# Residual tiles of both token halves kept on chip between output projection and channel mixer

## The chip, the cores and the metric

The kernel runs on one core of one Trainium2 chip. The metric is the device time of one execution in microseconds (us). Before the change three timed runs took 2567.0, 2571.26 and 2571.03 us, a median of 2571.03 us.

The engines are PE (TensorE, matrix products), DVE (VectorE), ACT (ScalarE), POOL (GpSimd) and SP (SyncE, which here only issues DMA transfers). Each engine works through its own list of instructions in order, and waits for the others by semaphores.

## The reference

A decoder trunk of two layers on one sequence of 1024 tokens with 1024 features, all in fp32. Each layer adds a token mixer and then a channel mixer to the residual stream `x`:

```
for layer in (0, 1):
    n = rms_norm(x, g1)
    x = x + mixer(n) @ w_out          # layer 0: dilated + forgetting attention, layer 1: differential attention
    n = rms_norm(x, g2)
    gate, up = split(n @ w_up, 2)     # 2816 columns each
    x = x + (silu(causal_conv3(gate)) * up) @ w_down
return rms_norm(x, g)
```

The change touches the two places where `x + mixer(n) @ w_out` ends and `rms_norm(x, g2)` begins.

## The kernel before

Activations lie transposed: a tile holds 128 features by 512 tokens. So the residual stream is eight feature tiles times two halves of the tokens (half 0 and half 1), 256 KB each. Every fp32 product is made of three matmuls, with operands split into a high and a low part (`mm3`, L150). Weights come in through `wget` (L119): a raw piece is loaded by SP into one of two `wr` slots, ACT makes the high part (`wh`, L129), DVE the low part (`wl`, L131). `split` (L162) does the same for activations, on ACT (L165) and DVE (L166). `put` (L193) is a load issued by SP, `store` (L196) a store issued by POOL; both queues work in order.

The order of the instructions comes from a scheduler: attention units and jobs of a list `J0` are woven together, and the tile pools decide by their slots when a tile can be filled.

`out_jobs` makes the jobs of the output projection. Its first job sums the first four head tiles into both token halves, the second job adds four more for half 0, and the job `rest` adds three more for half 1. After each product L1162 adds it to a residual tile `rt`, which had been loaded from DRAM (`parts`, `hp` in the traces), and POOL stores the tile there again. When half 0 is done, `stats` makes the norm's factors, and `blocks` loads the eight tiles of half 0 again (`t0`, `t<-hp`), multiplies each by the norm's factors (`token_blocks`, L1118 to L1121, an instruction at L1120), stores it to `half0` (`nt`) and splits it into `nh` and `nl`, the operands of the channel mixer.

`channel` is the channel mixer. It first adds the last head tile for half 1: eight products in a PSUM tile `dn`, added by L1364 to eight tiles `x` that are loaded from `parts` (`wq<-hp`). Each sum goes through `norm_chunk` (squares at L238, added up at L250) and is stored again (`hp<-wq`). `norm_cols` sums over the features with `ones` on PE (`small<-ones,sc`), `norm_rows` spreads the factor over the tokens (`dg`, `small<-dg`, `rb`). Then L1120 norms half 1, and L1384, L1385, L1393 and L1395 form the sums and differences with `b0`, the stored blocks of half 0, from which `cut` makes the split operands `bt` of the other block products (the up projection is done by seven block products in place of eight). Between these steps `lead` puts pieces of the gate product, whose sums ACT moves to `sc` (L931), POOL stores to `e` and SP loads again as `sc<-e` and `g<-e`. POOL also makes sums of raw up-projection weights in place (L824).

The channel mixer's pool has sixteen `wq` slots: before, `x` takes eight, `b0` four, and raw weights the rest; four more tiles of `b0` lie in `bt` slots. The pool `big` has 32 slots for `rt`, `t0`, `nh`, `nl`, the head tiles and others.

## Time and profile before

| | |
|---|---|
| median of three runs | 2571.03 us (2567.0 to 2571.26) |
| the profiled execution | 2565.89 us, of which its span takes 2564.1 us |
| mean granted TensorE clock | 0.983 of full speed |
| busy in the span | PE 96%, DVE 77%, ACT 48%, POOL 28% |
| DMA | 536.96 MB, 209 GB/s on average |

The profile is of one execution, 5.14 us shorter than the median. Its times count from the start of the span. A busy share is an average over the whole span; the passages between the stages are only seen in windows and timelines. In a timeline a row has its start, its length, the engine, line, operation, tiles and count, and in brackets how long the engine stood idle before it and what ended that.

### The profile page before, as it was taken

Reading aid. Unit: us, or ns where it says so; the run is one execution under the profiler, and the core shown is the slowest. Engines: PE = TensorE matmul, PEld = TensorE weight load, DVE = VectorE, ACT = ScalarE, POOL = GpSimd, SP = SyncE. Lnnn points to the kernel's source line nnn. Section 1 sums busy time; section 2 is a strip of 40 time slices with the busy share of each in tenths; the row PEclk is TensorE's granted clock in tenths of the full one; section 3 lists DMA queues with packets and bytes.
Section 4 is the critical chain, followed back from the end, with each engine's and each line's share of the span. In section 5 each row is a group of like instructions: output and inputs, shape, how many; then the busy total and the mean of one; then the engine's idle time right before and its main releaser. Section 6 shows DMA issues by size and latency. Waiting matters only on the chain.

```text
span 2564.1 us, 38450 instructions
## 1 busy us (share of the span) xinstructions
PE 2467.2 (96%) x12511; PEld 2047.6 (80%) x12511; DVE 1979.0 (77%) x3885; ACT 1221.5 (48%) x2443; POOL 721.4 (28%) x978
## 2 busy tenths in 40 slices
PE   8999999998899999999999999989888999999998
PEld 7899898776688888778888888877666888887886
DVE  7778878776988988775666888878769878977656
ACT  5456655454544344454434555545454443435433
POOL 1211112222444665100021211232225456740000
PEclk9999999998999999999999999999989999999998
DMA  5655556867766887664555555696576677766644
GB/s 192 229 172 172 178 173 216 255 204 275 216 207 219 244 241 240 205 220 167 193 202 169 197 182 193 203 288 216 179 253 198 204 238 242 248 201 231 226 130 160
DMA packets 249240, 536.96 MB, mean 209 GB/s; under 512 B 37976, under 2 KB 50896, under 8 KB 249040
## 3 DMA queue, kind: packets, MB, share of 16 engines
q1 hardware_dynamic: 179792, 320.02, 39.3%
q0 software_dynamic: 68672, 213.96, 25.1%
q8 instruction: 99, 1.62, 0.3%
q14 instruction: 101, 0.83, 0.1%
q10 hardware_dynamic: 576, 0.52, 0.1%
HBM read 362.33 MB, written 172.03 MB: 208 GB/s over the span
## 4 chain that ended last, share of the span: by engine, by line
PE 79%; DVE 8%; DMA 7%; ACT 3%; issue 2%; SPq 0%; POOL 0%; DVEq 0%; ACTq 0%; POOLq 0%
PE pj L145 67%; PE D L145 5%; PE O L145 4%; PE T L148 3%; DVE wl L131 2%; DMA wr<-in_wgate 1%; DVE bt L166 1%; PE small L145 1%; DMA wr<-in_wdown 1%; ACT wh L129 1%; DVE e L590 1%; DMA ncb<-cd 1%; ACT e L739 1%; DMA wr<-in_wqkC 1%; DMA ar<-td 1%
## 5 line engine op out<-in xcount | busy, mean ns | idle before, releaser
L145 PE MATMUL pj<-bt,wh 128*128 128x512 f32 x1760 | 554.2, 395 | 13.0 <-DVE bt L166 8.6
L145 PEld LDWEIGHTS pj<-bt,wh 128*128 128x128 f32 x1760 | 331.2, 188 | 93.5 <-DVE bt L166 11.6
L131 DVE TENSOR_TENSOR wl<-wr,wh 128x512 fp32r<-128x512 f32 (+2 forms) x340 | 235.7, 696 | 180.8 <-ACT wh L129 171.1
L145 PE MATMUL pj<-nh,wh 128*128 128x512 f32 x864 | 356.9, 413 | 16.8 <-ACT nh L232 8.6
L129 ACT ACTIVATE wh<-wr 128x512 fp32r<-128x512 f32 (+2 forms) x340 | 211.4, 624 | 290.5 <-PE pj L145 122.5
L145 PE MATMUL pj<-bt,wl 128*128 128x512 f32 x880 | 347.7, 395 | 0.0
L145 PE MATMUL pj<-nl,wh 128*128 128x512 f32 x864 | 346.2, 401 | 0.0
L145 PE MATMUL pj<-nh,wl 128*128 128x512 f32 x864 | 346.0, 401 | 0.0
L131 DVE TENSOR_TENSOR wl<-wq,wh 128x512 fp32r<-128x512 f32 x268 | 278.0, 1038 | 30.4 <-ACT wh L129 30.2
L129 ACT ACTIVATE wh<-wq 128x512 fp32r<-128x512 f32 x268 | 166.7, 628 | 239.2 <-PE pj L145 186.9
L824 POOL TENSOR_TENSOR wq<-wq 128x512 f32<-128x512 f32 x132 | 195.3, 1491 | 211.4 <-DVE wl L131 102.3
L145 PE MATMUL pj<-ah,wh 128*128 128x512 f32 (+1 forms) x628 | 248.0, 396 | 2.5 <-ACT s L1086 1.2
L145 PE MATMUL pj<-ah,wl 128*128 128x512 f32 (+1 forms) x628 | 246.2, 393 | 0.0
L145 PE MATMUL pj<-al,wh 128*128 128x512 f32 (+1 forms) x628 | 246.1, 392 | 0.0
L145 PEld LDWEIGHTS pj<-nh,wh 128*128 128x128 f32 x864 | 166.1, 192 | 49.9 <-ACT nh L232 8.6
L165 ACT ACTIVATE ph<-T 128x512 fp32r<-128x512 f32 (+3 forms) x288 | 138.9, 486 | 131.5 <-PE T L148 128.7
L145 PEld LDWEIGHTS pj<-bt,wl 128*128 128x128 f32 x880 | 165.8, 188 | 39.0
L145 PEld LDWEIGHTS pj<-nh,wl 128*128 128x128 f32 x864 | 165.5, 192 | 37.9 <-DVE wl L131 0.4
L145 PEld LDWEIGHTS pj<-nl,wh 128*128 128x128 f32 x864 | 166.2, 192 | 31.1 <-DVE nl L247 0.5
L166 DVE TENSOR_TENSOR pl<-T,ph 128x512 fp32r<-128x512 f32 (+3 forms) x288 | 157.5, 552 | 34.2 <-ACT ph L165 32.9
L148 PE MATMUL T<-ident,e 128*128 128x128 f32 x864 | 144.1, 277 | 19.2 <-DVE e L746 13.5
L145 PE MATMUL pj<-wh,nh 128*128 128x256 f32 (+1 forms) x512 | 149.0, 293 | 0.0
(476 smaller groups left out, 5339.7 us busy)
## 6 DMA issues: line engine op xcount, KB each, us to landing
wq<-in_wgate SPq DMA_DIRECT2D x88, 256.0 KB, 3.7
wq<-in_wup SPq DMA_DIRECT2D x88, 256.0 KB, 3.9
act<-v POOLq DMA_DIRECT2D x44, 512.0 KB, 3.6
td<-sc POOLq DMA_DIRECT2D x80, 256.0 KB, 4.5
wq<-in_wdown SPq DMA_DIRECT2D x80, 256.0 KB, 4.4
sd<-wq POOLq DMA_DIRECT2D x80, 256.0 KB, 4.1
ar<-td SPq DMA_DIRECT2D x80, 256.0 KB, 3.8
wr<-sd SPq DMA_DIRECT2D x80, 256.0 KB, 3.8
```

Of the source, the lines that this page charges most:

```text
L129: nc.scalar.activation(hi[:, :n], raw[:, :n], AF.Copy)
L131: nc.vector.tensor_tensor(lo[:, :n], raw[:, :n], f(hi[:, :n]), ALU.subtract)
L145: self.last = self.nc.tensor.matmul(*args, **kw)
L148: self.last = self.nc.tensor.transpose(*args)
L165: nc.scalar.activation(hi, src, AF.Copy)
L166: nc.vector.tensor_tensor(lo, src, f(hi), ALU.subtract)
L590: self.nc.vector.tensor_tensor_reduce(out=e[:, k0:k0 + w], in0=d[:, :w], in1=in1(k0, w), scale=1.0, scalar=init, op0=ALU.add, op1=ALU.min, ...
L739: nc.scalar.activation(e[m][:, :W], e[m][:, :W], AF.Exp, scale=-1.0, bias=nm[:, m:m + 1], accum_out=ls[:, m, i4:i4 + 1])
L824: nc.gpsimd.tensor_tensor(dst, x, y, op)
```

## The change

The tiles of both halves stay in SBUF. For half 0 the results of the second job are kept as `t0` and used by `blocks` directly; their store to `parts` stays. For half 1 the results of `rest` are kept as `self.t1[l]`, are no longer stored there, and are the `x` of `channel`. The eight tiles `b0` now all lie in `wq` slots. In each layer sixteen loads and eight stores of 256 KB go away; no arithmetic is added or removed. Lines behind the edit move by two, so L1162 becomes L1164, and L1364 becomes L1362.

```diff
-            def add(src, norm):
+            def add(src, keep=None):
...
-                    self.store(parts[l][m][:, cs[half]], t)
-                    if norm:
-                        self.norm_chunk(st, m, half, t, None)
+                    if half == 0 or keep is None:
+                        self.store(parts[l][m][:, cs[half]], t)
+                    if keep is not None:
+                        keep[m] = t
+                        if half == 0:
+                            self.norm_chunk(st, m, half, t, None)
                 return b, e
...
             def blocks():
-                ts = []
-                for m in range(10):
+                rest.fetch()
+                for m in range(9):
                     if m < 8:
-                        t = f(self.big.tile([P, HT], F32R, name="t0", tag="big"))
-                        self.put(t, parts[l][m][:, cs[0]])
-                        ts.append(t)
-                    if m == 0:
-                        rest.fetch()
-                    if 0 < m < 9:
-                        self.token_blocks(st, gi, 0, m - 1, ts[m - 1])
-                        self.store(half0[m - 1], ts[m - 1])
-                    if m > 1:
+                        self.token_blocks(st, gi, 0, m, t0[m])
+                        self.store(half0[m], t0[m])
+                    if m > 0:
                         hl = (self.big.tile([P, HT], F32R, name=x, tag="big") for x in ("nh", "nl"))
...
-            jobs += [self.job_out(w, [4, 5, 6, 7], [0], O, *add(part, True), 29 if l == 0 else 13)]
-            rest = self.job_out(w, [4, 5, 6], [1], O, *add(part, False), 27 if l == 0 else 14, 3)
+            jobs += [self.job_out(w, [4, 5, 6, 7], [0], O, *add(part, t0), 29 if l == 0 else 13)]
+            rest = self.job_out(w, [4, 5, 6], [1], O, *add(part, self.t1[l]), 27 if l == 0 else 14, 3)
...
-            x = [wq() for _ in range(8)]
-            for m in range(8):
-                self.put(x[m], parts[l][m][:, cs[1]])
+            x = [self.t1[l][m] for m in range(8)]
...
-            b0 = [wq() for _ in range(4)] + [f(small()) for _ in range(4)]
+            b0 = [wq() for _ in range(8)]
```

On SP's queue, at the start of layer 0's channel mixer, the lines with a minus are those of before (`hp` is the residual in DRAM, `nt` the stored blocks of half 0, `in_wgate` the gate weights):

```order
 L194 DMA cw<-in_cw 128x88
-L194 DMA wq<-hp_0_127 128x512
+L194 DMA wq<-nt_171 128x512
 L127 DMA wr<-in_wgate 128x512 x2
-L194 DMA wq<-hp_1_128 128x512
-L194 DMA wq<-hp_2_129 128x512
-L194 DMA wq<-hp_3_130 128x512
-L194 DMA wq<-hp_4_131 128x512
-L194 DMA wq<-hp_5_132 128x512
-L194 DMA wq<-hp_6_133 128x512
-L194 DMA wq<-hp_7_134 128x512
```

The reloads are gone and the first of the eight loads of half 0's blocks stands ahead of the first two weight pieces. Behind the blocks, before:

```order
L127 DMA wr<-in_wgate 128x512 x2
L194 DMA sc<-e_0_151 128x512
L194 DMA g<-e_1_152 128x512
L194 DMA wq<-in_wgate 128x512
L194 DMA wq<-in_wup 128x512
L127 DMA wr<-in_wgate 128x512 x2
```

And at the same place now:

```order
L127 DMA wr<-in_wgate 128x512 x2
L194 DMA wq<-in_wgate 128x512
L194 DMA wq<-in_wup 128x512 x2
L127 DMA wr<-in_wgate 128x512
L194 DMA sc<-e_0_151 128x512
L127 DMA wr<-in_wgate 128x512 x4
L194 DMA g<-e_1_152 128x512
```

Five weight pieces moved ahead of the load `g<-e_1_152`, and three raw weights ahead of the fifth piece.

On DVE, from the last residual adds of layer 0's channel mixer to its first L1120, before:

```order
L250 TENSOR_TENSOR sc_8020<-sc_8020,sc_8082 128x512
L178 TENSOR_SCALAR rq_x_8154<-small_8149 128x4
L183 TENSOR_TENSOR rq_z_8156<-rq_y_8155 128x4
L184 TENSOR_TENSOR rq_z_8156<-rq_z_8156,rq_x_8154 128x4
L185 TENSOR_SCALAR rq_z_8156<-rq_z_8156 128x4
L187 TENSOR_TENSOR rc_7487<-rq_y_8155,rq_z_8156 128x4
L131 TENSOR_TENSOR wl_8106<-wr_8102,wh_8104 128x512
L131 TENSOR_TENSOR wl_8127<-wr_8123,wh_8125 128x512
L273 TENSOR_SCALAR dg_8209<-ident_558,rc_7487 128x128 x4
L966 SCALAR_TENSOR_TENSOR pj_8663<-g_8146,cw_7953,pj_8663 128x512 x2
L1120 SCALAR_TENSOR_TENSOR wq_7999<-wq_7999,gn_69,rb_7503 128x512
```

The same stretch now:

```order
L250 TENSOR_TENSOR sc_7980<-sc_7980,sc_8042 128x512
L178 TENSOR_SCALAR rq_x_8114<-small_8109 128x4
L131 TENSOR_TENSOR wl_8129<-wr_8125,wh_8127 128x512
L183 TENSOR_TENSOR rq_z_8116<-rq_y_8115 128x4
L184 TENSOR_TENSOR rq_z_8116<-rq_z_8116,rq_x_8114 128x4
L185 TENSOR_SCALAR rq_z_8116<-rq_z_8116 128x4
L187 TENSOR_TENSOR rc_7487<-rq_y_8115,rq_z_8116 128x4
L131 TENSOR_TENSOR wl_8151<-wr_8147,wh_8149 128x512
L273 TENSOR_SCALAR dg_8169<-ident_558,rc_7487 128x128 x4
L131 TENSOR_TENSOR wl_8183<-wr_8179,wh_8181 128x512
L1120 SCALAR_TENSOR_TENSOR rt_7532<-rt_7532,gn_69,rb_7503 128x512
```

The convolution (L966) left the stretch for a place behind L1120, and the fifth, sixth and seventh weight splits since the start of the adds stand in it, where the third and fourth stood.

On DVE, where layer 1's first half is normed between the attention's last units (`e<-D` are logits, `pl` split probabilities), before:

```order
L1120 SCALAR_TENSOR_TENSOR t0_20492<-t0_20492,gn_69,rb_20468 128x512
L166 TENSOR_TENSOR nl_20497<-t0_20480,nh_20496 128x512
L166 TENSOR_TENSOR pl_20465<-T_20609,ph_20464 128x4x128
L166 TENSOR_TENSOR nl_20505<-t0_20488,nh_20504 128x512
L590 ISA e_20618,nm_20616<-D_20634,strip_14245,mn_20632 128x384
L590 ISA nm_20616 128x1
L166 TENSOR_TENSOR nl_20513<-t0_20492,nh_20512 128x512
L1120 SCALAR_TENSOR_TENSOR t0_20500<-t0_20500,gn_69,rb_20468 128x512
```

The end of the same run now:

```order
L1120 SCALAR_TENSOR_TENSOR rt_20080<-rt_20080,gn_69,rb_20428 128x512
L166 TENSOR_TENSOR nl_20469<-rt_20053,nh_20468 128x512
L1120 SCALAR_TENSOR_TENSOR rt_20119<-rt_20119,gn_69,rb_20428 128x512
L166 TENSOR_TENSOR nl_20475<-rt_20055,nh_20474 128x512
L1120 SCALAR_TENSOR_TENSOR rt_20172<-rt_20172,gn_69,rb_20428 128x512
L166 TENSOR_TENSOR nl_20481<-rt_20080,nh_20480 128x512
L166 TENSOR_TENSOR pl_20425<-T_20553,ph_20424 128x4x128
L166 TENSOR_TENSOR nl_20487<-rt_20119,nh_20486 128x512
L590 ISA e_20562,nm_20560<-D_20578,strip_14205,mn_20576 128x384
```

All eight L1120 and seven of the eight splits now stand ahead of the logits that before came after three L1120 and two splits; the run begins, as before, right behind another L590.

## Rows read from the trace of the kernel before

**Rows 1.** The page's busy times, with each engine's share of the span.

```profile
PE 2467.2 (96%) x12511; PEld 2047.6 (80%) x12511; DVE 1979.0 (77%) x3885; ACT 1221.5 (48%) x2443; POOL 721.4 (28%) x978
```

**Rows 2.** Windows: stretch, length, busy time per engine, clock, DMA share, GB/s.

```profile
579.00:593.00 14.00, 10.84 (x58) 8.50 (x58) 13.67 (x25) 8.78 (x18) 5.93 (x11) 0.94 0.82 289
614.00:650.00 36.00, 29.37 (x118) 22.46 (x116) 21.44 (x41) 16.78 (x30) 8.86 (x15) 0.91 0.88 314
650.00:695.00 45.00, 39.21 (x155) 30.08 (x156) 44.42 (x54) 24.79 (x45) 21.57 (x23) 0.92 0.71 211
700.00:1000.00 300.00, 300.00 (x1295) 243.09 (x1294) 262.04 (x352) 121.74 (x199) 173.56 (x190) 1.00 0.74 229
1819.00:1836.00 17.00, 9.65 (x47) 6.85 (x46) 16.72 (x39) 10.04 (x25) 5.93 (x11) 0.83 0.53 192
1868.00:1906.00 38.00, 29.51 (x110) 22.23 (x110) 21.11 (x39) 17.85 (x31) 10.94 (x17) 0.87 0.86 307
1906.00:1950.00 44.00, 39.28 (x159) 30.77 (x158) 43.79 (x58) 24.52 (x45) 18.25 (x20) 0.92 0.65 203
```

**Rows 3.** Timeline of SyncE's queue, both passages: start, length, line, transfers issued.

```profile
615.61 0.98 SPq L127 DMA_DIRECT2D wr<-in_wgate  x2
616.64 4.83 SPq L194 DMA_DIRECT2D wq<-hp  x7
...
628.54 1.78 SPq L127 DMA_DIRECT2D wr<-in_wgate  x2
...
640.58 0.33 SPq L194 DMA_DIRECT2D g<-e  x1
...
641.97 0.84 SPq L127 DMA_DIRECT2D wr<-in_wgate  x2
...
1871.22 0.86 SPq L127 DMA_DIRECT2D wr<-in_wgate  x2
...
1883.99 1.02 SPq L127 DMA_DIRECT2D wr<-in_wgate  x2
```

**Rows 4.** DMA, 612 to 640: GB/s in 40 slices, then issues with us to landing.

```profile
GB/s 0 0 0 0 0 84 185 287 222 307 266 255 249 307 389 395 389 418 395 407 398 407 404 418 410 410 416 407 404 418 398 415 407 407 398 445 386 395 366 220
...
wq<-hp SPq DMA_DIRECT2D x8, 256.0 KB, 6.6
...
wr<-in_wgate SPq DMA_DIRECT2D x4, 256.0 KB, 10.5
```

**Rows 5.** Timeline of DVE, both passages; idle time before in brackets.

```profile
619.30 0.69 DVE L1364 TENSOR_TENSOR wq<-wq,pj 128x512 f32<-128x512 f32 x1 [3.52 <-DMA wq<-hp]
...
630.02 2.27 DVE L250 TENSOR_TENSOR sc<-sc 128x512 f32<-128x512 f32 x3
...
645.62 1.83 DVE L1120 SCALAR_TENSOR_TENSOR wq<-wq,gn,rb 128x512 f32<-128x512 f32 x1
...
1873.96 0.69 DVE L1364 TENSOR_TENSOR wq<-wq,pj 128x512 f32<-128x512 f32 x1 [2.48 <-DMA wq<-hp]
...
1886.11 2.27 DVE L250 TENSOR_TENSOR sc<-sc 128x512 f32<-128x512 f32 x3
...
1905.13 2.24 DVE L1120 SCALAR_TENSOR_TENSOR wq<-wq,gn,rb 128x512 f32<-128x512 f32 x2 [1.24 <-ACT rb L282]
```

**Rows 6.** Timeline of PE: column sums of layer 0, norm stretch of layer 1.

```profile
632.48 1.80 PE L145 MATMUL small<-ones,sc 128*128 128x1 f32 x8
...
1831.30 0.87 PE L148 MATMUL T<-ident,e 128*128 128x128 f32 x3 [4.46 <-DVE e L746]
```

**Rows 7.** Timeline of DVE where layer 1's first half is normed.

```profile
1819.74 2.07 DVE L1120 SCALAR_TENSOR_TENSOR t<-t,gn,rb 128x512 f32<-128x512 f32 x3
...
1823.53 0.61 DVE L590 CUSTOM_DVE_ANT_0 e<-D,strip,mn 128x384 f32<-128x384 f32 x1
```

**Rows 8.** Timelines of DVE and of POOL (GpSimd), layer 1's channel mixer.

```profile
1933.19 5.33 DVE L166 TENSOR_TENSOR bt<-wq,bt 128x512 fp32r<-128x512 f32 x1
...
1933.81 4.15 POOL L824 TENSOR_TENSOR wq<-wq 128x512 f32<-128x512 f32 x3
```

More of the change, by code (lines that the diff above doesn't have):

```diff
@@ L1149, in run @@
         cs = [slice(hf * HT, (hf + 1) * HT) for hf in range(2)]
+        self.t1 = {}
         def out_jobs(l, w, base):
             st, gi, O = stF[l], 2 * l + 1, Os[l]
-            def add(src, norm):
+            def add(src, keep=None):
                 def b(m, half):
@@ L1174, in blocks @@
             def blocks():
-                ts = []
-                for m in range(10):
+                rest.fetch()
+                for m in range(9):
                     if m < 8:
-                        t = f(self.big.tile([P, HT], F32R, name="t0", tag="big"))
-                        self.put(t, parts[l][m][:, cs[0]])
-                        ts.append(t)
-                    if m == 0:
-                        rest.fetch()
-                    if 0 < m < 9:
-                        self.token_blocks(st, gi, 0, m - 1, ts[m - 1])
-                        self.store(half0[m - 1], ts[m - 1])
-                    if m > 1:
+                        self.token_blocks(st, gi, 0, m, t0[m])
+                        self.store(half0[m], t0[m])
+                    if m > 0:
                         hl = (self.big.tile([P, HT], F32R, name=x, tag="big") for x in ("nh", "nl"))
-                        st["h"][m - 2, 0], st["l"][m - 2, 0] = hl
-                        self.split(st["h"][m - 2, 0], st["l"][m - 2, 0], ts[m - 2])
+                        st["h"][m - 1, 0], st["l"][m - 1, 0] = hl
+                        self.split(st["h"][m - 1, 0], st["l"][m - 1, 0], t0[m - 1])
                 yield 0.0
+            t0, self.t1[l] = {}, {}
             last = lambda k: 4 * k + 3 if l == 0 else 2 * k + 1
@@ L1193, in out_jobs @@
             jobs = [self.job_load(O, k, last(k)) for k in range(4)]
-            jobs += [self.job_out(w, [0, 1, 2, 3], [0, 1], O, *add(base, False), last(3))]
+            jobs += [self.job_out(w, [0, 1, 2, 3], [0, 1], O, *add(base), last(3))]
             jobs += [self.job_load(O, k, last(k)) for k in range(4, 6)]
-            jobs += [self.job_out(w, [4, 5, 6, 7], [0], O, *add(part, True), 29 if l == 0 else 13)]
-            rest = self.job_out(w, [4, 5, 6], [1], O, *add(part, False), 27 if l == 0 else 14, 3)
+            jobs += [self.job_out(w, [4, 5, 6, 7], [0], O, *add(part, t0), 29 if l == 0 else 13)]
+            rest = self.job_out(w, [4, 5, 6], [1], O, *add(part, self.t1[l]), 27 if l == 0 else 14, 3)
             jobs += [Job(stats, 1.3), Job(blocks, 0.0)]
```

## The prediction

> **What bounds the kernel now.** I read the page's busy times first. PE is busy for 96% of the span [rows 1], so only places where PE waits or runs at a low clock can give anything; the reader should look for those places, not at totals. The windows show where they are not: from 700 to 1000, inside a channel mixer, PE is busy all 300 us at a granted clock of 1.00, with 1295 matmuls, that is 0.232 us each [rows 2]. They are at the two passages from a mixer to its channel mixer. Layer 0: 6.6 of 36 us idle from 614 to 650 (36.00 − 29.37) and 5.8 of 45 from 650 to 695, at clocks 0.91 and 0.92. Layer 1: 8.5 of 38 from 1868 to 1906 and 4.7 of 44 from 1906 to 1950, at 0.87 and 0.92 [rows 2]. The idle sums to 25.6 us; the missing clock, (1 − clock) × length, to 3.2 + 3.6 + 4.9 + 3.5 = 15.2 us. These 41 us are all that a better passage could return.
>
> Two stretches lie just ahead, where the first half is normed: 579 to 593 and 1819 to 1836, PE idle 3.2 and 7.4 us, with DVE busy 13.67 of 14 and 16.72 of 17 us [rows 2]. There DVE is the limit.
>
> Then who is waited for. SyncE's queue in layer 0: two raw weights (`wr`) at 615.61, seven of the eight `wq<-hp` from 616.64 over 4.83 us; the next pair of raw weights is issued at 628.54 and the third at 641.97, behind a `g<-e` at 640.58. In layer 1 the first two pairs stand at 1871.22 and 1883.99 [rows 3]. The reloads take 6.6 us each and the weights beside them 10.5, with the DMA engines moving some 400 GB/s in the second half of that window [rows 4]. On DVE the first residual add (L1364) starts at 619.30 after 3.52 us for `wq<-hp`, and at 1873.96 after 2.48; the sums of squares (L250) end at 630.02 + 2.27 = 632.3 and 1886.11 + 2.27 = 1888.4; the second half's first norm (L1120) starts at 645.62 and 1905.13 [rows 5]. PE sums the columns at 632.48, right behind [rows 6]. What follows the norm is DVE's alone: 44.42 of 45 us and 43.79 of 44 busy [rows 2]. So an earlier L1120 moves the whole tail of the passage.
>
> **The change, part by part.** No instruction of an engine's arithmetic is added or removed; 16 loads and 8 stores of 256 KB go in each layer.
>
> *Second half.* Eight reloads leave SyncE's queue and the adds work on tiles that are already there. DVE is free at 619.30 − 3.52 = 615.8 and 1873.96 − 2.48 = 1871.5 [rows 5]. By the new order eight adds, seven L250 and about four weight splits stand until the last sum: 19 × 0.68 us = 12.9, the length of an add there [rows 5], so 628.7 and 1884.4: 3.6 and 4.0 us earlier than now. From there to L1120 it took 13.3 and 16.7 us. Left in it are the eight column products (1.8 us, rows 6), 19 and 24 gate matmuls that now stand between them and the spread of the result, at 0.23 us, or 0.46 if the clock is half, and some 2.5 us of spreading: 8.7 to 13 and 9.8 to 15.3. Without any wait for weights L1120 would come 4 to 8 us earlier in layer 0 and 5 to 11 in layer 1.
>
> But weights are waited for: there are two `wr` slots, and in the new order seven splits stand before L1120 in layer 0 where four did, six in layer 1 as before. A pair follows the one before after 628.54 − 615.61 = 12.9, then 13.4 us (the second stood behind the reloads, the third behind `g<-e`), and after 12.8 in layer 1 [rows 3]. Two megabytes less in front of it are 2.1 MB / 400 GB/s = 5.2 us; and `g<-e` now stands behind five more weight loads. I put the round at 6.5 to 7.5 us: 5.3 to land (10.5 − 5.2, rows 4) and 1.3 for the two halves of a split, at 0.68 each. The seventh split's load is issued three rounds after 615.6, so it is there at 615.6 + 3 × 6.5 + 5.3 = 640.4, and L1120 at about 641: 5 us earlier. Layer 1 needs the sixth: 1871.2 + 2 × 7.5 + 5.3 + 2 = 1893.5 to 1895: about 10 us. I take **−5** (0 to −9) and **−10** (−5 to −13). DVE's idle time there, 36 − 21.44 = 14.6 and 38 − 21.11 = 16.9 us [rows 2], leaves room for both.
>
> *First half.* The eight reloads of the blocks go too; DVE was full there all the same [rows 2], so I cost them at nothing. What changes is DVE's order: eight L1120 and up to eight splits now stand in one run, where logits (L590) stood between them. In layer 1 the logits at 1823.53 come after a run that starts at 1819.74 [rows 7]; five instructions stood between, sixteen will: 11 × 0.66 us later (2.07 for three, rows 7), to 1830.8. PE waits there now until 1831.30, 4.46 us, for DVE [rows 6]. In layer 0 the shift is three instructions, 2 us. DVE is full in both stretches whatever the order, so the run's end is not later; I take **+1** for both together, between −2 and +6 (the whole shift of 7.3 on PE, less 1 of cover).
>
> *Smaller parts.* The dropped stores of the second half lay beside work: nothing on DVE or PE waits for a store's issue there. The first half's blocks now have eight `wq` slots and eight of sixteen are free for raw weights, so some sums of weights on GpSimd (L824) come earlier; their number is the same, and I cost it at nothing: if the cover goes, see the third rival. The residual tiles hold `big` slots longer; DVE's and ScalarE's orders show no new wait for one.
>
> Sum: −5 − 10 + 1 = −14 us, from −22 to −7 for this case. The profiled execution took 2565.89 us, 5.1 less than the median of 2571.03; I apply the difference to the median: **2557 us**, own range 2549 to 2564.
>
> **The rivals.**
> *Weights come as slowly as now* (slower): rounds of 13 us, because the transfers of the first half's blocks and of the weights saturate the engines without the reloads too [rows 4]. The seventh split would be there at 615.6 + 39 + 5.3 + 1 = 661, L1120 15 us later in layer 0, and no earlier in layer 1: +16, 2587 us. It decides from a round of 7.9 us on in layer 0: 615.6 + 3 × 7.9 + 6.3 = 645.6, today's time. Against it: one of the two long rounds was a wait for `g<-e`, which moves behind.
>
> *The reload is largely hidden*: rounds of 9 us give layer 0 +3, layer 1 −7, and +1 for the first half: −3, 2568 us. For it: DVE's wait for the first reload was only 3.52 and 2.48 us [rows 5], and the weights took longer to land than the reloads.
>
> *GpSimd's sums fall on the norm chain.* At 1933.19 one split `bt<-wq,bt` took 5.33 us, where an instruction of that shape takes 0.68, and GpSimd ran three sums from 1933.81 over 4.15 us [rows 8]. One such stop on L250 or a weight split in each layer costs 2 × 4.65 = 9.3, and −14 becomes −5: 2566 us. Against it: the three sums in a row need raw weights that are loaded later than the norm chain. The Trainium skill's page SBUF — State Buffer, section "Who interferes with whom", says that a VectorE instruction with two inputs in SBUF and a GpSimd instruction that reads SBUF exclude each other for a whole instruction, while one that reads PSUM and one SBUF operand does not contend. By that rule L250 and the splits can be stopped and the adds L1364, which read PSUM, cannot: 2566 us with the sums there, 2557 without. By the rows alone the adds might stop too.
>
> *More than I count*: with weights and adds both early PE closes most of its gaps and the clock stays up. Two thirds of the 41 us give −27, 2544 us; all of it would be 2530. Against: DVE stays full after L1120.
>
> **How the numbers follow.** Two runs of one kernel differ by up to 0.2% here, 5 us, so I call changes inside that none. Forecast 0.60 (faster); slow weights 0.07 (slower); hidden reload 0.13 (none, a third of it just faster or slower); sums on the chain 0.10 (half faster, half none); more than counted 0.10 (faster). Faster 0.77, none 0.15, slower 0.08. From 2541 to 2568 lie the forecast, the third rival, most of the second and half of the last: about eight in ten.
>
> **What would show it.** In the changed profile: the first add in each layer starts without a wait for a load and PE does six or seven of the residual products in a row; the column products stand some 4 us earlier; the pairs of `wr` loads stand 6.5 to 7.5 us apart; L1120 some 5 and 10 us earlier; PE's idle time from 614 to 650 and from 1868 to 1906 about halved; and the total is shorter by what the layers show. I am wrong if L1120 waits for a weight split at the old time, if DVE shows splits of several us beside GpSimd's sums in the norm chain, or if PE's wait near 1823 to 1831 grows by more than 5 us and carries to the end.

## The result and the profile after

The changed kernel took 2542.27 us (median of 4 runs, 2540.54 to 2549.05) against 2571.15 (4 runs, 2567.00 to 2576.09): ratio 0.9892, 95% interval 0.9867 to 0.9917. Measured again on another occasion, beside three of the experiments, it took 2546.62 us (5 runs) against 2567.99: 0.9914 (0.9901 to 0.9928). So it is faster by 21 to 29 us, not by the 14 forecast. The first value lies inside the range on record (2541 to 2568), near its low end, and below the forecast's own 2549 to 2564.

The profiled execution took 2549.05 us, 16.8 less than the profiled one of before. The busy times on the page moved by less than 1% against [rows 1], since no arithmetic was removed; what the 12.7 us of PE are is told behind the table of stages:

```profile
PE 2454.5 (96%) x12511; PEld 2043.8 (80%) x12511; DVE 1965.0 (77%) x3885; ACT 1220.7 (48%) x2443; POOL 722.1 (28%) x962
```

The windows at the two passages, columns as in [rows 2]; in layer 1 they are taken 10 us earlier, as everything there has moved:

```profile
614.00:650.00 36.00, 29.88 (x121) 23.93 (x120) 23.22 (x43) 16.26 (x30) 9.77 (x14) 0.86 0.81 282
650.00:695.00 45.00, 39.50 (x161) 30.77 (x160) 43.68 (x53) 23.46 (x43) 27.70 (x23) 0.96 0.65 200
1858.00:1896.00 38.00, 30.31 (x129) 23.47 (x128) 24.53 (x43) 15.47 (x30) 14.41 (x20) 0.96 0.89 307
1896.00:1940.00 44.00, 36.98 (x145) 28.90 (x145) 42.94 (x54) 24.19 (x44) 24.20 (x19) 0.88 0.58 188
```

PE is idle there for 6.1, 5.5, 7.7 and 7.0 us (length less the first number), 26.3 in all, where it was 25.6 before. The gain is thus not smaller gaps in the passages: the stages end sooner. SyncE's queue shows what is gone (columns as in [rows 3]): first the output weights of layer 0, then layer 0's passage, then layer 1's:

```profile
546.13 27.65 SPq L127 DMA_DIRECT2D wr<-in_woA  x9
...
609.14 0.94 SPq L127 DMA_DIRECT2D wr<-in_wgate  x2
610.13 5.12 SPq L194 DMA_DIRECT2D wq<-nt  x7
615.35 1.07 SPq L127 DMA_DIRECT2D wr<-in_wgate  x2
...
626.13 0.33 SPq L127 DMA_DIRECT2D wr<-in_wgate  x1
...
627.36 12.96 SPq L127 DMA_DIRECT2D wr<-in_wgate  x4
...
1855.82 0.86 SPq L127 DMA_DIRECT2D wr<-in_wgate  x2
...
1864.55 1.61 SPq L127 DMA_DIRECT2D wr<-in_wgate  x2
```

No `hp` is read; the nine output weights stand in one row. Before, reloads stood among them, and the queue waited at a reload (`L194`) for the store of the tile (`hp<-rt`). Two rows of the kernel before, and below them a row from the view of the queue's waits from 545 to 600, with the total, the number and the longest:

```profile
558.35 0.33 SPq L194 DMA_DIRECT2D t<-hp  x1
560.95 17.10 SPq L127 DMA_DIRECT2D wr<-in_woA  x5
```

```profile
SPq L194 <- DMA hp<-rt: 7.7, 3, 3.4
```

Of the eight reloads three stood among the weights and waited, five came behind them; in layer 1 (1770 to 1830) it was again three waits, 7.2 us. After the change there is none. DVE, answering to [rows 5] (the adds are now L1362):

```profile
610.94 1.37 DVE L1362 TENSOR_TENSOR rt<-rt,pj 128x512 f32<-128x512 f32 x2 [1.62 <-PE pj L145]
...
640.11 1.41 DVE L1120 SCALAR_TENSOR_TENSOR rt<-rt,gn,rb 128x512 f32<-128x512 f32 x2
...
1856.17 1.28 DVE L1362 TENSOR_TENSOR rt<-rt,pj 128x512 f32<-128x512 f32 x2
...
1881.69 1.41 DVE L1120 SCALAR_TENSOR_TENSOR rt<-rt,gn,rb 128x512 f32<-128x512 f32 x2
```

The adds wait for no load. The second half's first norm (L1120) stands 5.5 us earlier in layer 0 and 23.4 in layer 1. PE, answering to [rows 6], with the waits that the closed run of norms was expected to cause:

```profile
567.82 0.58 PE L145 MATMUL small<-ones,o 128*128 128x1 f32 x4 [0.34 <-DVE o L250]
...
583.44 1.12 PE L148 MATMUL T<-ident,e 128*128 128x128 f32 x4 [4.91 <-DVE pl L166]
...
1770.84 0.61 PE L145 MATMUL small<-dg,ones 128*128 128x128 f32 x4
...
1802.24 0.50 PE L145 MATMUL small<-ones,nacc 128*128 128x1 f32 x4
...
1819.07 1.12 PE L148 MATMUL small<-ident,Ra 128*128 128x128 f32 x4 [7.58 <-DVE pl L166]
```

Such marks cut each profile into stages, and one table then serves all experiments. For layer 0: A, from the program's first column sums (41.1 here) to the first half's (567.82); B, from there to the second half's first L1120 (640.11); C, the norm tail, from there to DVE's L950, the sum that ends the first chunk's gate (693.55). For layer 1: D, from the last `small<-dg` before it (1770.84) to the first half's column sums (1802.24); E to L1120 (1881.69); F to L950 (1939.20). Three stretches are left out: the start (39 to 41 us), what lies between layer 0's tail and D (1076 to 1083) and what follows F (605 to 609). Stages in us, from one profile each:

| kernel | A | B | C | D | E | F | sum | median ratio to before |
|---|---|---|---|---|---|---|---|---|
| before | 529.6 | 75.4 | 56.3 | 34.6 | 92.6 | 53.1 | 841.5 | |
| after | 526.7 | 72.3 | 53.4 | 31.4 | 79.5 | 57.5 | 820.8 | 0.9892 |
| after, again (e5) | 526.5 | 72.4 | 53.7 | 31.3 | 78.5 | 57.9 | 820.2 | 0.9914 |
| e1 first half kept | 526.3 | 73.2 | 58.1 | 31.2 | 93.5 | 54.2 | 836.6 | 0.9974 |
| e2 second half kept | 529.6 | 69.1 | 54.6 | 34.8 | 82.2 | 56.1 | 826.4 | 0.9948 |
| e3 reload by GpSimd | 524.7 | 76.5 | 56.2 | 32.8 | 93.5 | 54.2 | 837.9 | 0.9991 |
| e4 third weight slot | 526.2 | 72.6 | 52.4 | 31.5 | 83.2 | 51.5 | 817.3 | 0.9901 |
| e6 idle reloads, 1st half | 529.1 | 72.5 | 53.9 | 36.2 | 78.4 | 54.6 | 824.6 | 0.9953 |
| e7 run opened | 526.8 | 69.7 | 53.6 | 31.5 | 80.0 | 55.1 | 816.6 | 0.9918 |
| e8 twelve free slots | 526.9 | 71.8 | 51.5 | 31.6 | 79.6 | 53.6 | 815.0 | 0.9883 |
| e9 sums left out | 526.1 | 71.7 | 47.1 | 31.5 | 79.6 | 48.3 | 804.3 | 0.9849 |
| e10 stores kept | 526.5 | 74.7 | 54.2 | 31.6 | 84.2 | 56.0 | 827.2 | 0.9953 |
| e11 and idle loads, 2nd half | 525.4 | 73.5 | 53.5 | 32.5 | 86.1 | 57.1 | 828.1 | 0.9957 |
| e12 sixteen free slots | 526.7 | 71.9 | 52.8 | 31.6 | 78.3 | 56.8 | 818.0 | 0.9899 |

The two profiles of the changed kernel agree within 1.0 us in each stage. Its six stages are 21 us shorter than before's: A −2.9, B −3.1, C −2.9, D −3.2, E −13.1, F +4.4. The stretches that are left out are 4 us longer, which leaves the 16.8 us of the profiled executions.

Over the span PE's idle time is 96.9 us before and 92.8 after (span less busy time), while its busy time fell by 12.7 us with the same 12511 matmuls. Windows over B and E, before and then after, show where (columns as in [rows 2]):

```profile
570.23:645.62 75.39, 67.37 (x303) 53.74 (x304) 49.83 (x106) 32.76 (x61) 18.92 (x36) 0.86 0.73 254
1812.56:1905.13 92.57, 71.60 (x318) 55.43 (x317) 58.49 (x131) 41.38 (x91) 21.40 (x38) 0.89 0.64 228
```

```profile
567.82:640.11 72.29, 61.24 (x294) 49.97 (x295) 49.95 (x107) 33.55 (x63) 16.39 (x29) 0.88 0.56 199
1802.24:1881.69 79.45, 62.61 (x313) 50.08 (x312) 57.05 (x133) 40.02 (x89) 18.04 (x30) 0.94 0.53 188
```

PE is busy 6.1 and 9.0 us less there. A few matmuls have moved behind the mark (9 and 5 fewer records); and of the matmuls of 512 columns 43 and 42 took over 0.35 us before, 22 and 11 after, where 0.23 is usual at full clock [rows 2].

### The profile page after: what moved, and what is told of

Same layout as the page of the kernel before. It is cut to its first block, busy times and chain, and to the rows that moved or that the text cites. A ratio compares the mean times of both kernels' runs of the same rounds, so it can differ in the third digit from the quotient of the medians.

```text
span 2547.3 us, 38327 instructions
## 1 busy us (share of the span) xinstructions
PE 2454.5 (96%) x12511; PEld 2043.8 (80%) x12511; DVE 1965.0 (77%) x3885; ACT 1220.7 (48%) x2443; POOL 722.1 (28%) x962
## 4 chain that ended last, share of the span: by engine, by line
PE 77%; DMA 7%; DVE 7%; issue 5%; ACT 2%; POOL 1%; SPq 0%; ACTq 0%; DVEq 0%; POOLq 0%
PE pj L145 64%; PE D L145 5%; PE O L145 4%; PE T L148 3%; DMA wr<-in_wdown 1%; DVE wl L131 1%; PE small L145 1%; DMA ar<-act 1%; DMA wr<-in_wgate 1%; DMA ncb<-cd 1%; DVE bt L166 1%; DVE e L590 1%; ACT wh L129 1%; DVE rt L1120 1%; ACT e L739 1%
## 5 line engine op out<-in xcount | busy, mean ns | idle before, releaser
L131 DVE TENSOR_TENSOR wl<-wq,wh 128x512 fp32r<-128x512 f32 x268 | 269.5, 1006 | 33.6 <-ACT wh L129 33.5
L824 POOL TENSOR_TENSOR wq<-wq 128x512 f32<-128x512 f32 x132 | 204.3, 1552 | 216.3 <-DVE wl L131 112.9
L166 DVE TENSOR_TENSOR pl<-T,ph 128x512 fp32r<-128x512 f32 (+3 forms) x288 | 157.8, 552 | 34.0 <-ACT ph L165 32.5
L148 PE MATMUL T<-ident,e 128*128 128x128 f32 x864 | 144.1, 277 | 19.5 <-DVE e L746 9.4
```

The source lines that it names most:

```text
L131: nc.vector.tensor_tensor(lo[:, :n], raw[:, :n], f(hi[:, :n]), ALU.subtract)
L148: self.last = self.nc.tensor.transpose(*args)
L166: nc.vector.tensor_tensor(lo, src, f(hi), ALU.subtract)
L824: nc.gpsimd.tensor_tensor(dst, x, y, op)
```

## The experiments

The kernel before was timed beside each group: 2568.97 us for e1 to e4, 2567.99 for e5 to e8, 2570.32 for e9 to e12.

**e1 and e2: each half alone.** Of the changed kernel, e1 lets the second half be stored and loaded as before, e2 the first:

```diff
 e1
-            rest = self.job_out(w, [4, 5, 6], [1], O, *add(part, self.t1[l]), 27 if l == 0 else 14, 3)
+            rest = self.job_out(w, [4, 5, 6], [1], O, *add(part), 27 if l == 0 else 14, 3)
-            x = [self.t1[l][m] for m in range(8)]
+            x = [wq() for _ in range(8)]
+            for m in range(8):
+                self.put(x[m], parts[l][m][:, cs[1]])
-            b0 = [wq() for _ in range(8)]
+            b0 = [wq() for _ in range(4)] + [f(small()) for _ in range(4)]
 e2
-                        self.token_blocks(st, gi, 0, m, t0[m])
+                        t = f(self.big.tile([P, HT], F32R, name="t0", tag="big"))
+                        self.put(t, parts[l][m][:, cs[0]])
...
```

> Only the half-0 part: the blocks use the kept tiles, half 1 is stored and reloaded as before, and the mixer's pool as before. Theory A (from the trace after): the half-0 reloads cost by their place in SyncE's queue, where eight of them stand among the loads of output weights; taking them out brings the half-0 norm 5.4 us earlier in layer 0 (579.21 to 573.78) and some 3 in layer 1, and most of that reaches the end: 6 to 12 us faster than before, about 2560 to 2565. Theory B (the prediction's): these reloads cost nothing and the closed run of norms costs 1 us: within 3 us of before.

> Only the half-1 part: its tiles stay on chip (no stores by the last job, no reloads by the mixer, all of the blocks in wq slots), while half 0 is reloaded for its norm as before. Theory A: the gain of the change is about half here, 12 to 18 us, and the half-0 norm stays at about 579 us in layer 0. Theory B: all of the gain of the change is here, so it measures as the whole change, 26 to 30 us faster than before.

Measured: e1 2563.12 us (8 runs), ratio 0.9974 (0.9962 to 0.9986), that is −6.7 us by the ratio (the medians differ by 5.9); e2 2556.68 (5 runs), 0.9948 (0.9935 to 0.9960), −13.4 (12.3). Theory A held for both, in e1 at its low end, except that e2's first norm of the first half came at 575.8 and not at 579. Together −20, against −21 to −29 for the whole change. So the second half is worth about what the prediction gave it, though not for its reasons (below), and the first half, costed at nothing, is worth a third of the whole. In the table e1 shortens A and D, e2 B and E. e2 also has the blocks in `wq` slots, which e1 hasn't: e8 below bears on that.

**e3: the kernel before, with the first half's reload issued by GpSimd.**

```diff
-                        self.put(t, parts[l][m][:, cs[0]])
+                        self.store(t, parts[l][m][:, cs[0]])
```

> The kernel before, with the sixteen half-0 reloads issued by GpSimd in place of SyncE; every byte still moves. Theory A (the place in SyncE's queue is what costs): the output weights come as early as in the changed kernel, and 3 to 10 us are gained, nearly as much as by keeping half 0 on chip. Rival (the round trip itself costs: the store must land before the load): no gain, within 3 us of before, or a loss, as GpSimd's queue now waits for each store.

Measured: 2566.06 us (11 runs), 0.9991 (0.9979 to 1.0004): no change that can be told. A and D shrink (−4.9, −1.8), since the weights are free; B grows by 1.1 and E by 0.9. In its DVE timeline the norms now wait for the reloads themselves:

```profile
576.05 0.75 DVE L1120 SCALAR_TENSOR_TENSOR t<-t,gn,rb 128x512 f32<-128x512 f32 x1 [1.07 <-DMA t<-hp]
...
584.68 0.75 DVE L1120 SCALAR_TENSOR_TENSOR t<-t,gn,rb 128x512 f32<-128x512 f32 x1 [1.69 <-DMA t<-hp]
```

Another queue moves the wait; only not reloading removes it.

**e4: a third slot for raw weights** in the passage, paid for with one `sc` slot:

```diff
+                if self.w3 and self.wnext % 3 == 2:
+                    raw = self.fp.tile([P, HT], F32, name="wr", tag="wr3", bufs=1)
+                else:
                     raw = self.wp.tile([P, PC], F32, name="wr", tag="wr", bufs=self.wraw)
...
-            self.nwq, self.nsc, self.ng, self.nbt = 16, 8, 2, 24
+            self.nwq, self.nsc, self.ng, self.nbt = 16, 7, 2, 24
...
```

> The changed kernel with a third slot for raw weights while the mixer begins, paid for by one sc slot fewer (seven for eight). Theory A: the two slots set the pace after the change: DVE's waits for weight splits (4.1 us at 625.41 in layer 0, 3.4, 3.2 and 4.1 at 1872.55, 1878.14 and 1887.18 in layer 1) go or halve, 4 to 10 us faster than the changed kernel, 32 to 38 faster than before. Rival: DVE is full behind the norm of half 1 anyway, and the weights are no more than a shift of waits: within 3 us of the changed kernel, 26 to 31 faster than before.

Measured: 2543.38 us (4 runs), 0.9901 (0.9887 to 0.9914), the same as the whole change. B is 72.6, E even 83.2. The waits of Theory A did not go: in layer 0 ScalarE waits 4.91 us for the third gate weight to land, 4.52 without the third slot. The number of slots is not what holds the second half's norm; the landing of the weights stays in front of it (below).

**e5: the whole change again.** 2546.62 us (5 runs), 0.9914 (0.9901 to 0.9928).

> The whole change once more, unaltered, beside the three kernels that vary it, so that they are compared on one chip. Theory (the two halves add up, with a little more together): ratio 0.988 to 0.992, 2540 to 2549 us against 2569 before. Rival (the first result was a lucky set of runs, and the two halves give only their sum, 20 us): about 0.9922, with an interval that excludes 0.989. Its profile is the second of this kernel: what differs between the two profiles by itself is the grain of all comparisons of single profiles; I expect the marks up to the second half's first norm to repeat within 1 us and the channel mixers to differ by some us.

The interval leaves out 0.989 and includes the sum of the halves, as the rival has it, though it overlaps with that of the first measurement: that the halves give more together than their sum is not shown. The marks repeat as expected.

**e6: the first half's reloads back in the queue, with nobody waiting for them.**

```diff
...
                     if m < 8:
+                        self.put(ghost[l][m], parts[l][m][:, cs[0]])
                         self.token_blocks(st, gi, 0, m, t0[m])
```

> The whole change, but the eight loads of the first half's residual come back in each layer on SyncE's queue at their old places, as copies from the residual's DRAM buffer to a DRAM buffer that nobody reads. No engine waits for the data; what is back is the place in the queue ahead of the output weights (each copy waits there until its tile has been stored) and the traffic. Theory Q (the first half's gain, some 7 us, is the queue: output weights stood behind reloads that waited for stores): the column sums and the first norm of the first half go back to their old times, 570 and 579 in layer 0, and 5 to 8 us of the 27 are lost, ratio 0.992 to 0.994. Theory D (the gain is that the norm no longer waits for reloaded data): the norm starts as in the whole change, 574, and the time is that of the whole change within 2 us, ratio 0.988 to 0.991.

Measured: 2554.91 us (6 runs), 0.9953 (0.9937 to 0.9970), 8.3 us above the whole change beside it. Theory Q held in A and D, which go back to 529.1 and 36.2, and nearly in its size (8.3 us where 5 to 8 were expected). Its time for layer 0's norm was too pessimistic (574.9, not 579). SyncE's queue, layer 1:

```profile
1796.81 7.63 SPq L194 DMA_DIRECT2D gh<-hp  x3
1804.54 0.53 SPq L127 DMA_DIRECT2D wr<-in_woC  x1
```

The copy at 1796.81 and its two followers hold the queue for 7.6 us, and the next output weight is issued behind them. But e6 holds the queue more than the kernel before did, as its copies all stand among the weights. Its waits for stores from 545 to 600:

```profile
SPq L194 <- DMA hp<-rt: 14.4, 8, 4.8
```

That is 14.4 us in eight waits for 7.7 in three, and 18.1 in seven for 7.2 in three in layer 1. So e6 shows that copies in the queue cost time with nobody waiting for their data; its 8.3 us are not the price of the reloads of before, for which e1's 6.7 is nearer.

**e7: the closed run of first-half norms opened.**

```diff
-                yield 0.0
+                    yield 0.6 if m < 8 else -4.8
```

> The whole change with the closed run of first-half norms and splits broken up: the job that issues them gives way after each block, so that logits and residual adds stand between them again, as with the reloads of before; its share of the plan is taken back at its end, so that the rest of the order is nearly as it was. Theory (the closed run costs PE the 4.9 and 7.6 us that it waits at 583 and 1819, but DVE is full there, so that this comes back as the same work later): those waits of PE shrink to under 3 us each and the time is the same within 3 us, ratio 0.987 to 0.991. Rival R (PE's waits there are on the path): 6 to 12 us faster than the whole change, ratio 0.984 to 0.987. Rival S (the split tiles come later and the second half waits for them): slower than the whole change by 3 us or more.

Measured: 2548.66 us (5 runs), 0.9918 (0.9903 to 0.9933): no difference from the whole change that these runs can tell. PE's wait of 7.58 us becomes 5.05 and 2.04, that of 4.91 becomes 4.32 and 1.95, not under 3 each; the order of the second half's norms moved a little too. The waits are not on the path for their length.

**e8 and e12: where the first half's blocks lie.** The change had moved four of the eight from the split tiles' slots (`bt`) to `wq`. e8 moves those four back, e12 moves all eight:

```diff
-            b0 = [wq() for _ in range(8)]
+            b0 = [wq() for _ in range(4)] + [f(small()) for _ in range(4)]   (e8)
+            b0 = [f(small()) for _ in range(8)]                             (e12)
```

> The whole change with one edit undone: four of the eight first-half blocks go to the slots of the split tiles again, as before, so that four slots fewer are free for raw weights and GpSimd's sums of weights come later. Theory (the edit only makes the slots come free earlier; the sums of weights are not what the passage waits for): same as the whole change within 2 us, and GpSimd's sum at 1907 that took 8.65 us moves later or stands beside other work. Rival G (GpSimd's sums beside DVE's splits cost the 10 us that layer 1 gives back after its first norm): the sums come after the splits, DVE's four splits at 672 take about 2.6 us instead of 9.3, and the kernel is 4 to 10 us faster than the whole change. Rival W (raw weights become late): 4 us slower or more.

> The whole change with all eight first-half blocks in the slots of the split tiles: sixteen slots are free for raw weights, where the whole change has eight and the run with four blocks there had twelve (8 us faster). Theory (more free slots let the sums of weights run earlier, while DVE waits for the norm anyway): as fast as with twelve or up to 5 us faster, ratio 0.986 to 0.989. Rival (split tiles now wait for the blocks' slots, 32 pairs of tiles over 24 slots): L166 waits in the norm tail and the gain is lost, ratio 0.990 or more.

Measured: e8 2538.31 us (4 runs), 0.9883 (0.9867 to 0.9899), 8.3 us under the whole change beside it. It is the only version that computes everything, is faster than that one and has an interval clear of its (0.9901 to 0.9928), if only just; from the first measurement (0.9867 to 0.9917) it is not clear. e12 2546.31 (5 runs), 0.9899 (0.9883 to 0.9916), no better than the whole change as far as this can tell. The first expectation had the sign of the slots wrong (e8 frees slots), as the second says. C and F are 2.2 and 4.3 us shorter in e8 than in the run of the whole change beside it, 0.9 and 1.1 in e12.

**e9: GpSimd's sums of weights left out** for three chunks in each layer:

```diff
+                    if fc > 2:
                     sum_(R[fc, "11"], R[fc, "11"], R[fc, "21"], ALU.subtract)
```

and likewise for the other two sums of a chunk.

> The whole change without GpSimd's sums of weights for the first three chunks of the channel mixer in each layer (the raw weights are used as they are, so that part of the computation is left out; their loads stay, the accumulating load too). Theory G (beside DVE's splits these sums stop DVE: in the changed profile four splits of 672.01 take 9.33 us and five instructions of 1916.81 take 14 us, where 0.68 each is usual): all instructions of 670 to 690 and 1915 to 1930 take 0.68 us, the gate's sum L946 comes 5 to 9 us earlier in each layer and the kernel is 8 to 16 us faster than the whole change, ratio 0.985 to 0.988 if that is 2546. Rival (DVE runs ahead of PE there, the stops are absorbed): within 3 us of the whole change. The edit that gave four blocks to the split tiles' slots again, which frees four slots for raw weights (my earlier expectation had that the wrong way round) and moves the sums earlier, gained 8 us: more than that here would say that it removed only a part.

Measured: 2530.41 us (5 runs), 0.9849 (0.9831 to 0.9867), 16 us under the whole change as measured again. In the profile after, DVE and below it GpSimd in layer 0's tail:

```profile
670.30 0.68 DVE L943 TENSOR_TENSOR sc<-sc,pj 128x512 f32<-128x512 f32 x1
670.90 1.19 DVE L131 TENSOR_TENSOR wl<-wr,wh 128x512 fp32r<-128x512 f32 x1
672.01 9.33 DVE L166 TENSOR_TENSOR bt<-rt,bt 128x512 fp32r<-128x512 f32 x4
...
663.49 8.04 POOL L824 TENSOR_TENSOR wq<-wq 128x512 f32<-128x512 f32 x1 [2.57 <-DMA wq<-in_wgate]
```

and DVE in e9 (two lines further down in the code):

```profile
670.62 0.69 DVE L131 TENSOR_TENSOR wl<-wq,wh 128x512 fp32r<-128x512 f32 x1 [1.09 <-ACT wh L129]
671.23 5.03 DVE L166 TENSOR_TENSOR bt<-rt,bt 128x512 fp32r<-128x512 f32 x2
676.19 0.67 DVE L947 TENSOR_TENSOR sc<-sc,pj 128x512 f32<-128x512 f32 x1
```

Theory G held in the time and in L950 (C −6.6, F −9.6 against e5), not in the detail that all instructions take 0.68 us: the sums of later chunks still stop two splits. The edit takes away a second thing too: after the change ScalarE waits once in each tail for a sum of weights, 8.02 us at 679.59 and 8.76 at 1924.00, and not at all in e9. How much of the 16 us is DVE's stops and how much that wait, no run separates.

**e10 and e11: the second half's transfers back, with nobody waiting for the data.** e10 stores the second half's residual as before; e11 also loads it again, into a buffer in DRAM:

```diff
-                    if half == 0 or keep is None:
+                    if True:                                                (e10, e11)
                         self.store(parts[l][m][:, cs[half]], t)
...
             x = [self.t1[l][m] for m in range(8)]
+            for m in range(8):                                              (e11)
+                self.put(ghost[l][m], parts[l][m][:, cs[1]])
```

> The whole change with the eight stores of the second half's residual back in each layer (2 MB that nobody reads). Theory (they lie beside work, as the prediction says): within 2 us of the whole change. Rival (the transfers delay the last attention's loads and the weights at the passage): 3 to 8 us slower.

> As the run with the stores kept, and the eight loads of the second half's residual back on SyncE's queue too, as copies into a DRAM buffer that nobody reads; the adds still use the tiles on chip. Theory A (the second half's 13 us are made by the queue and the traffic in front of the weights): the weights behind the copies come late again, the first norm of the second half goes back by 4 us or more in layer 0 and by 8 or more in layer 1, and 8 to 13 us are lost against the run with the stores kept. Theory B (they are made by the adds that no longer wait for reloaded data): the adds start as in the whole change, at most 4 us are lost.

Measured: e10 2558.77 us (6 runs), 0.9953 (0.9938 to 0.9967); e11 2560.53 (6 runs), 0.9957 (0.9942 to 0.9972). Against the second measurement of the whole change (0.9914) the stores alone cost 0.0039 of the time, 10 us (5 to 15 from the two intervals), at or above what the rival gave them (3 to 8), and against the first more; the whole change was not timed beside them; the loads behind them 0.0004, which can't be told from nothing. Theory B of e11 held. ScalarE's timeline in layer 1 after the change, then in e10:

```profile
1840.42 0.63 ACT L129 ACTIVATE wh<-wr 128x512 fp32r<-128x512 f32 x1 [1.03 <-DMA wr<-in_wgate]
1844.09 1.29 ACT L129 ACTIVATE wh<-wr 128x512 fp32r<-128x512 f32 x2 [3.04 <-DMA wr<-in_wgate]
1845.28 0.58 ACT L759 ACTIVATE Ra<-O 128x512 f32<-128x512 f32 x1
```

```profile
1849.62 0.63 ACT L129 ACTIVATE wh<-wr 128x512 fp32r<-128x512 f32 x1 [4.30 <-DMA wr<-in_wgate]
1854.27 0.63 ACT L129 ACTIVATE wh<-wr 128x512 fp32r<-128x512 f32 x1 [4.02 <-DMA wr<-in_wgate]
...
1855.72 0.58 ACT L759 ACTIVATE Ra<-O 128x512 f32<-128x512 f32 x1
```

With the stores ScalarE waits 8.3 us for two gate weights instead of 4.1, and the exit of the last attention (L759), on which PE waits, stands behind these conversions in its order. The profile before shows the same two waits, 4.72 and 2.86 us. That the weights land later because the stores share the DMA engines with them is the reading that fits; no run separates that from the queue that issues the stores.

## Why the prediction was right and wrong

**Where time could be won** held: every gain lies at the two passages and just ahead of them.

**Second half, −5 and −10.** The marks came almost as told, in layer 0 by luck: L1120 stands at 640.1, where about 641 was forecast. To see why, take the split of the last head's output, with which the passage begins; before and then after:

```profile
614.47 1.30 DVE L166 TENSOR_TENSOR o<-wr,o 128x512 fp32r<-128x512 f32 x2
1870.17 1.30 DVE L166 TENSOR_TENSOR o<-wr,o 128x512 fp32r<-128x512 f32 x2
```

```profile
608.02 1.30 DVE L166 TENSOR_TENSOR o<-wr,o 128x512 fp32r<-128x512 f32 x2
1854.77 1.30 DVE L166 TENSOR_TENSOR o<-wr,o 128x512 fp32r<-128x512 f32 x2
```

From there to L1120 it takes 32.1 us in layer 0, where it took 31.1: the passage itself gained nothing, it begins 6.4 us earlier. In layer 1 it takes 26.9 for 35.0, a gain of 8.0 where 10 were forecast; the rest of E's 13.1 lies ahead of the split.

Two steps of the sum were wrong. *"I put the round at 6.5 to 7.5 us"*, with 5.3 for a load to land: the pairs follow after 6.2, 10.8 and 8.1 us in layer 0 and twice 8.7 in layer 1, and a load of layer 0's second pair takes 9.9 to land. In layer 0 that and the early begin, which was not forecast, cancel: the seventh weight is issued 25.1 us after the first, not 19.5. It was not the 2 MB in front of the weights either: with them back in the queue (e11) the pairs follow after 6.0 to 10.8 us. And in layer 0 that landing stands in front of the norm; ScalarE, then PE, after the change:

```profile
624.75 0.63 ACT L129 ACTIVATE wh<-wr 128x512 fp32r<-128x512 f32 x1 [4.52 <-DMA wr<-in_wgate]
```

```profile
627.66 0.79 PE L145 MATMUL pj<-nh,wh 128*128 128x512 f32 x1 [5.35 <-ACT sc L931]
```

The last square (L238, at 626.51) and the copy that PE waits for (L931) stand behind this conversion in ScalarE's order, and the column sums behind both. A third slot doesn't change that (e4).

*"The dropped stores of the second half lay beside work: nothing on DVE or PE waits for a store's issue there"*: true of the issue, but not of the time. The stores are worth some 10 us (e10): B 2.3 to 2.4 us and E 4.7 to 5.7 longer with them, nearly all of it ahead of the split, the rest being spread over stages that vary by as much. What the queue's reloads added on top of them was nothing that can be measured (e11). From e11 to before the passage differs by 7.7 us in layer 1 (27.3 and 35.0) and not in layer 0 (31.6 and 31.1). That is what adds that need no reloaded data are worth, together with the changed order; the two were not tried apart.

**First half, "I cost them at nothing" and +1.** This term was set at nothing and is worth a third of the gain. The sentence looked at DVE, which was full during the norms, and not at what stood behind the reloads in SyncE's queue: the output projection's own weights. Three reloads in each layer waited there, 7.7 and 7.2 us, until their tiles had been added and stored, and the next weights were issued behind them. A and D shorten by 2.9 and 3.2 us (e1: 3.3 and 3.4); e1 gives −6.7 us in all, and e6 takes 8.3 back with nothing but the queue and the traffic, in a stronger dose. The data matter as well: with the queue freed but the data still reloaded (e3) nothing is won.

**The closed run** came as expected: in layer 1 the logits (L590, at 1819.53) follow the first L1120 (1809.41) after 10.1 us instead of 3.8 [rows 7], 6.3 later where 7.3 were worked out, and PE waits 7.58 us instead of 4.46 [rows 6]. In the end it costs nothing that can be measured: opened (e7), the time is the same (0.9918 and 0.9914, each give or take 0.0015). The +1 held as far as that tells.

**GpSimd's sums, "I cost it at nothing".** The number of sums is the same and they cost DVE much the same: counting DVE's instructions longer than 1 us behind the second half's first L1120, up to 720 and 1985, the time beyond 0.68 each is 15.6 and 18.3 us before, 14.8 and 14.8 after, 5.3 and 4.6 without the sums of three chunks (e9). Beside each of them GpSimd runs such a sum. The third rival named the right lock at the wrong place: not on the norm chain (no L250 was stretched there, and one weight split, at 1878.14, took 1.40 us) but in the tail, where DVE stood full in [rows 2]. It is no cost that the change brought, but a reserve: 16 us for three chunks of sums, with ScalarE's waits for them (e9). The step is mis-sized, if at all, by the one edit that bears on it: four blocks moved to `wq`, which e8 undoes for −8 us, just clear of the noise. Why twelve free slots do better than eight and than sixteen is shown only in part: the tails C and F shrink by 6.5 us in e8, with two sums instead of three beside DVE's splits, and e12 keeps little of that.

**The tail.** The prediction let an earlier L1120 move the whole tail. C does (−2.9 more), F does not: 53.1 us became 57.5, so layer 1 gave 4.4 of its gain back. In e8 it is 53.6.

**The rivals.** *Weights as slow as now* fell with the result (L1120 at 640.1 and not at 661), and *reload largely hidden* with e2, which alone gave −13.4 us, although the rounds of 9 us that it supposed are nearer to the truth than the forecast's. *More than I count* (2544) is where the time landed, for half of its reason: PE's gaps in the passages are as long as they were, but in B and E the granted clock is higher and PE's busy time 15 us shorter. So it is partly luck that the result lies in the range on record: the range reached so far down only for this rival.

**The Trainium skill's rule.** The page SBUF — State Buffer, section "Who interferes with whom", says that a VectorE instruction with two SBUF inputs and a GpSimd instruction that reads SBUF exclude each other, while VectorE with one input in PSUM does not contend. The runs agree with both. In e12 GpSimd started a sum at 1901.60 while DVE ran instructions with two SBUF inputs back to back:

```profile
1901.60 14.53 POOL L824 TENSOR_TENSOR wq<-wq 128x512 f32<-128x512 f32 x1 [2.42 <-DMA wq<-in_wgate]
```

```profile
1914.90 0.67 DVE L943 TENSOR_TENSOR sc<-sc,pj 128x512 f32<-128x512 f32 x1
1915.50 1.18 DVE L131 TENSOR_TENSOR wl<-wr,wh 128x512 fp32r<-128x512 f32 x1
```

It ended at 1916.13, 1.23 us behind the start of L943, the first DVE instruction there that reads PSUM (`pj`); the shortest sums of the trace take 1.27. The sum of 663.49 above ends at 671.53, 1.24 us behind the start of the L943 of 670.30. There are eleven sums of 7 us or more in eight of the fourteen profiles, and each ends 1.23 to 1.25 us behind the start of such an add, the only one beside it. The DVE instruction behind the add is then the one that is stretched, to 1.18 us in e12 and 1.19 here.

**What stays open**: whether the stores act through the DMA engines or through GpSimd's queue; what of layer 1's passage is the reloaded data and what the order; how e9's 16 us divide; why e8 is better than e12; and 5 to 8 us between the two measurements of the whole change. The fastest version that computes all of it is e8, 2538.31 us.

## What to carry to other kernels

A reload that nobody seems to wait for still has a place in an in-order queue: read what stands behind it, and whether it waits for a store there. A store that nobody waits for still has bytes: look at the loads that land beside it and at the engine that waits for those. To price such transfers, keep them and take away their consumer, and check that the queue then waits as often and as long as it did; to price a wait, do the opposite. When a mark comes at the forecast time, measure it from the start of its stage too: in layer 0 the right time was two errors that cancelled.

## What was not expected of the hardware

A GpSimd sum of two 128x512 tiles, mostly 1.3 to 1.7 us, took 7.1 to 14.5 us in eleven cases, beside an unbroken run of DVE instructions with two SBUF inputs, and ended only behind one that reads PSUM. The other way round, one split of 0.68 us took 4.36 us (layer 1 after the change, at 1921.38) beside a run of three sums that lasted 4.08. So one engine can be held off for a whole run of the other's instructions, and not for one alone. It isn't so each time: after the change a sum at 1890.50 came in between two such DVE instructions and it was DVE that stood, GpSimd and then DVE:

```profile
1890.50 1.60 POOL L824 TENSOR_TENSOR wq<-wq 128x512 f32<-128x512 f32 x1
```

```profile
1890.14 0.68 DVE L1383 TENSOR_TENSOR v<-rt,wq 128x512 f32<-128x512 f32 x1
1890.75 1.91 DVE L131 TENSOR_TENSOR wl<-wr,wh 128x512 fp32r<-128x512 f32 x1
```

What decides which of the two gets in is not shown.
